# A streaming encoder step: one more gate pair by seven products, four convolution rows as filling, the last pair stored raw

## The chip, the cores and the metric

The kernel runs on one core of a Trainium2 chip. The metric is the device time of one execution in microseconds (us), lower is better. The median of three runs is 1542.54 us (1541.74 to 1542.68).

Engines by the profile's names: PE is TensorE (matmuls), PEld its weight load, DVE VectorE, ACT ScalarE, POOL GpSimd, SP SyncE, which issues the DMAs. Each works through its own instructions in order.

## The reference

One layer: a root-mean-square norm, one input projection whose columns feed an attention branch, a short convolution and two sets of sigmoid gates; the branches are merged by the gates, then an output projection, an MLP and a gated embedding follow. 1024 prompt rows and 32 sample rows (T = 1056), width 1024, all in float32.

```python
h = rmsnorm(x, g_mix)
proj = h @ w_in                     # columns: q k v cb cc cx (512 each), ga gc (1024 each)
q, k, v, cb, cc, cx, ga, gc = jnp.split(proj, SPLITS, axis=-1)
y_attn = attend(q, k, v).reshape(b, t, SB_WIDTH) @ w_attn_out
conv_out, new_buf = causal_conv(cc * cx, conv_buf, conv_w)     # width 3, per channel
y_conv = (cb * conv_out) @ w_conv_out
merged = jax.nn.sigmoid(ga) * y_attn + jax.nn.sigmoid(gc) * y_conv
x = x + merged @ w_o
...

def stick_breaking(q, k, v, q_pos, k_pos):
    z = jnp.einsum('bqhd,bkhd->bhqk', q, k) * scale
    mask = k_pos[None, :] < q_pos[:, None]
    log_1m = jnp.where(mask, jax.nn.log_sigmoid(-z), 0.0)
    tail = lax.cumsum(log_1m, axis=3, reverse=True) - log_1m
    a = jnp.where(mask, jnp.exp(jax.nn.log_sigmoid(z) + tail), 0.0)
    return jnp.einsum('bhqk,bkhd->bqhd', a, v)
```

## The kernel before

Activations lie with features on the partitions and the 1056 rows along the free axis. Every operand is split into a high and a low part, and each product of a weight block with an activation block is three matmuls: high by high, high by low, low by high. The high part is a cast on ACT, the low part a subtraction on DVE.

**Stages.** In-projection, attention (64 steps), branches, output projection, MLP (up, down), gated embedding. The change touches the first three. The norm's factor `rs` is multiplied in after the in-projection.

**In-projection.** The columns form blocks of 128, taken in pairs (a "set"): gates g0 to g15 (0 to 7 are the attention branch's, 8 to 15 the convolution branch's), q, k, v and the three convolution parts cb, cc, cx (four blocks each). Gates g0 to g3 come first, by plain products (`first_gates`). The sets from index 2 of `SETS` on go by seven products of half-size blocks in the place of eight (`seven`): 7 products x 2 column halves x 12 matmuls of 128x264 = 168 for a pair. A product is a step of the loop `run`; after each step, `run` lets every generator in `side` do one piece of its work. A set has 14 such steps. In `side` are: `prepare`, which forms the weight sums of the next set (four sums on POOL, L203) and splits them (L164 on ACT, L166 on DVE); the fetch of the set after; and what `follow` puts there once a set is done: scaling by `rs` (L482), for gates the sigmoid (L578) and the store to `gd` in DRAM (L579, `gate_done`), for cx and cb the steps of the convolution (`conv_in`: the product with cc, L539, the taps, L547 on ACT and L155 on DVE; `conv_gate`: L563, the cast L567, its low part L570). `follow` gives the second block of a pair a later start than the first, by a table of steps: six for cx, four for cb.

In `seven` the last product of a set (A22, `ps_A11i<-T,shA_i` in the profile) overwrites the PSUM tile that L257 on DVE reads, and its results are copied by ACT (L651).

**What is left of the gates is filling.** The six gate blocks that no set makes (10 to 15) are cut into pieces (`plan_gates`; a quarter of the columns of one block is 24 matmuls of 128x264 in four pieces, L659 to L661, its copy L663). Behind them in the plan stand the embedding products (`embed_pieces`, L752 to L754, copied by ACT at L755) and the first `CFILL` = 2 rows of the convolution branch (`conv_pieces`, L975 to L977, 36 matmuls of 128x352 a row, multiplied by the gate on DVE at L979). `START` = 3 units of the plan (72 matmuls) run between the in-projection and attention; the others are dealt to the attention steps by `shares`, which spreads the plan's total over the steps. A filling group takes one of two PSUM tiles.

**Attention.** A step n makes scores for 128 queries (L791, L792, into the one score tile `z`), reads them by a sigmoid on ACT (L795), masks on POOL (L802), scans on DVE (L809), transposes two steps later (L845, copied at L848 on ACT and L849 on DVE) and multiplies with the values (L866). `ORDER = "LSAFBFG"` is the order of these in a step; F is filling. At the last step the score tile becomes two more filling tiles (`zf`).

**Branches.** For each of the 8 rows of each branch that no filling made: 36 matmuls of 128x352, times the gate, merged. `READY` names the gates that are in DRAM scaled and with their sigmoid; for the others `branch_scale` and `branch_sigmoid` do it here (for the convolution branch the scaling is on POOL, for the attention branch on DVE).

PE, ACT, DVE and POOL run in the order in which the code is written (`manual_schedule`); SP's order is made by a scheduler. Buffers of `bpool` (34) serve nearly everything of size 128x1056.

Of the kernel before, what the change touches and what calls it, by code (L numbers as in the profile page):

```python
# [37 lines left out]
SHB = 4  # L38
AT1 = (5, 4, 6, 7, 8, 12)
AT_IN = (4, 8, 10, 12, 14, 18)  # L40
READY = (4, 5, 6, 7, 8, 9)
CFILL = 2
ORDER = "LSAFBFG"
START = 3
MM = {mybir.EngineType.Activation, mybir.EngineType.PE, mybir.EngineType.DVE, mybir.EngineType.Pool}
# [3 lines left out]
def tile_step(  # L49
# [8 lines left out]
    nc = tc.nc  # L58
# [79 lines left out]
    raws, ws, side = {}, {}, []  # L138
# [134 lines left out]
    def after(n, *gens):  # L273
        for _ in range(n):
            yield
        for g in gens:
            yield from g
# [12 lines left out]

    goff = (3 * SB + 3 * CW) // P
    coff = 3 * SB // P
    SETS = [("g", 0), ("g", 2)] + [(nm, 0) for nm in ("cc", "cx", "cb", "q", "k", "v")] + [("g", 4)]
    SETS += [(nm, 2) for nm in ("q", "k", "v")] + [("g", 6)] + [(nm, 2) for nm in ("cc", "cx", "cb")] + [("g", 8)]
    base = {"g": goff, "q": 0, "k": 4, "v": 8, "cb": coff, "cc": coff + 4, "cx": coff + 8}
    xw = [[blk(f"x{h}{j}", F32, [P, 2, TH]) for j in range(4)] for h in range(2)]

# [14 lines left out]
    def fetch_in(s_):  # L312
        nm, n = SETS[s_]
        fetch_pair(f"i{s_}", w_in, base[nm] + n)
# [113 lines left out]
    gd = dpool.tile([16, P, T], F32, name="gd")  # L428
# [153 lines left out]
    def follow(nm, n, ms, wait=0):  # L582
        gens = []
        for p, m in zip((n, n + 1), ms):
            if nm in "qk":
                gens.append(keys_or_queries(nm, p, m))
            elif nm == "v":
                gens.append(values(p, m))
            elif nm == "cc":
                cst["cc", p] = m  # L590
                gens.append(call(scaled, m))
            else:
                gens.append({"cx": conv_in, "cb": conv_gate, "g": gate_done}[nm](p, m))
        side.extend([after(wait, gens[0]), after(wait + {"v": 6, "cx": 6, "cb": 4, "g": 3}.get(nm, 1), gens[1])])

    def first_gates():

# [318 lines left out]
    def gate_ready(b):  # L916
        return b[1] + (8 if b[0] == "c" else 0) in READY

# [63 lines left out]
    def plan_rest():  # L982

        es = [(n, embed_pieces(n)) for n in range(KD)]
        cs = [(n, conv_pieces(n)) for n in range(CFILL)]
        e_, c_ = 4 * KD, 12 * CFILL
        i0, ne, nc_ = len(plan), 0, 0
# [17 lines left out]

    SEQ_B = [("c", CFILL)]
    for n in range(KD):
        SEQ_B += [("a", n), ("c", n + CFILL + 1)] if n < KD - CFILL - 1 else [("a", n)]

# [65 lines left out]
        for p in range(4):  # L1075
            nc.scalar.copy(sampled[1][p // 2][:, p % 2, PAST:], ksT[p])

    plan_gates([n for n in range(4, 16) if n not in READY])
    plan_rest()
    total = sum(size for size, _ in plan)  # L1080
    place, done = min(hooks), 0.0
# [27 lines left out]
    with tc.manual_schedule(engines=MM):  # L1109
        nc.scalar.preload_act_table_set("sqrt_and_others")  # L1110
        run(first_gates())
        for s_ in range(2, len(SETS)):
            nm, n = SETS[s_]
            if s_ == 2:
                side.append(after(1, stats_x()))
            elif s_ == 4:
                nc.scalar.preload_act_table_set("sigmoid_and_others")
            if s_ + 1 < len(SETS):
                side.append(prepare(f"i{s_ + 1}", AT_IN))
            else:  # L1120
                side.extend([after(4, second_parts(0)), after(6, second_parts(1)), after(4, call(hooks_to, -20)), after(10, call(hooks_to, 0))])
            if s_ + 2 < len(SETS):
                side.append(after(5, call(fetch_in, s_ + 2)))
            m = blk(f"m1_i{s_}"), blk(f"m2_i{s_}")
            run(seven(f"i{s_}", *m, copy_of))
            follow(nm, n, m, 6 * (s_ == 2))
        keys_values(0, 0)
        run(ahead(START))
        while side:
            run(range(1))  # L1130
# [97 lines left out]
    with tc.manual_schedule(engines=MM):  # L1228
        queries(0, 0, 0)
        queries(0, 0, 1)  # L1230
        for n in range(LAST + 3):
# [5 lines left out]
            if n < LAST:  # L1237
                i = steps[n][2]
# [671 lines left out]
    with tc.manual_schedule(engines=MM):  # L1910
# [35 lines left out]
        for u in range(ND):  # L1946
            v = u + 4
# [147 lines left out]
```

## Time and profile before

| what | us |
|---|---|
| median of three runs | 1542.54 |
| the profiled execution | 1542.94 |
| its span in the profile | 1541.1 |
| in-projection, up to the last product of the last set | 0 to 373.4 |
| attention, first scores to last values | 382.6 to 594 |
| DMA, mean busy share of 16 queues | 0.51 |

A row of a timeline has the start, the duration, the engine, the line, the operation, what is written and read, and in brackets how long the engine had been idle before it and what ended that. A row of groups has the count, the busy time with the mean in ns, and the idle time. A row of windows has the stretch, its length, each engine's busy time with its count of instructions, the granted PE clock (1.00 is full), the DMA share and GB/s. Matmuls overlap in the pipeline: one of 128x264 is listed with 0.28 us, while the next starts 0.12 us later. So PE's pace is read from starts and from counts.

### The profile page before, as it was taken

The page shows a single profiled execution, that of the slowest core. Times are in us where ns is not written, and L with a number is a line of the kernel's source. Part 1 is how long each engine was busy: PE and PEld are TensorE (multiplying, and loading weights), DVE is VectorE, ACT ScalarE, POOL GpSimd, SP SyncE. Part 2 cuts the span into 40 slices and gives each one's busy share as a digit, 9 for nine tenths or more (in the row PEclk, how much of TensorE's full clock was granted, in tenths as well). Part 3 has the DMA queues.
Part 4 walks back from the last instruction along what each step waited for, and adds up shares of the span by engine and source line. Part 5 has one row for each costly group of instructions (what it writes and reads, how often), then busy time and mean ns, then how long its engine had stood idle before and what let it go on. Part 6 is the DMA issues. An engine that isn't in the chain of part 4 may idle for free. (4 is left out here: it accounts for less than half of the span.)

```text
span 1541.1 us, 29464 instructions
## 1 busy us (share of the span) xinstructions
PE 1522.7 (99%) x11840; PEld 1511.4 (98%) x11840; DVE 1056.5 (69%) x1425; ACT 747.3 (48%) x1367; POOL 335.1 (22%) x342
## 2 busy tenths in 40 slices
PE   8999999999999999999999999999999999999997
PEld 8999999999999999999999999999999999999997
DVE  7568656656777887665577555445577986789756
ACT  6544444434555664322365555555643334434654
POOL 2123322230222232101312222222020220000253
PEclk9999999999999999999999999999999999999999
DMA  6513545415644843354354343444886897683443
GB/s 221 202 53 111 192 153 193 166 45 182 197 117 151 281 141 133 133 180 176 121 188 152 140 154 137 142 148 154 290 289 199 286 326 237 210 273 122 138 129 117
DMA packets 110569, 268.96 MB, mean 175 GB/s; under 512 B 12992, under 2 KB 30144, under 8 KB 110432
## 3 DMA queue, kind: packets, MB, share of 16 engines
q1 hardware_dynamic: 110144, 266.75, 51.2%
q8 instruction: 93, 1.52, 0.4%
q14 instruction: 44, 0.36, 0.1%
q10 hardware_dynamic: 288, 0.32, 0.1%
HBM read 186.31 MB, written 80.72 MB: 173 GB/s over the span
## 5 line engine op out<-in xcount | busy, mean ns | idle before, releaser
L1690 PE MATMUL ps_dn<-fh,whi_dn 128*128 128x264 f32 x896 | 254.7, 284 | 0.0
L1691 PE MATMUL ps_dn<-fl,whi_dn 128*128 128x264 f32 x896 | 254.5, 284 | 0.0
L1692 PE MATMUL ps_dn<-fh,wlo_dn 128*128 128x264 f32 x896 | 254.5, 284 | 0.0
L1692 PEld LDWEIGHTS ps_dn<-fh,wlo_dn 128*128 128x128 f32 x896 | 168.7, 188 | 0.0
L1691 PEld LDWEIGHTS ps_dn<-fl,whi_dn 128*128 128x128 f32 x896 | 168.5, 188 | 0.0
L1690 PEld LDWEIGHTS ps_dn<-fh,whi_dn 128*128 128x128 f32 x896 | 168.5, 188 | 0.0
L809 DVE TENSOR_TENSOR_SCAN r<-r 128x128 f32<-128x128 f32 (+3 forms) x64 | 86.6, 1353 | 5.6 <-POOL r L802 5.6
L203 POOL TENSOR_TENSOR s_i<-raw_i,raw_i 128x512 f32<-128x512 f32 x30 | 41.2, 1372 | 223.7 <-DVE slS_i L166 194.0
L203 POOL TENSOR_TENSOR s_u<-raw_u,raw_u 128x512 f32<-128x512 f32 x30 | 44.1, 1471 | 184.6 <-DVE slS_u L166 184.4
L1577 ACT CAST whi_dn<-raw_dn 128x1024 fp32r<-128x1024 f32 x40 | 42.1, 1051 | 84.7 <-PE ps_dn L1691 84.7
L802 POOL TENSOR_SCALAR_AFFINE_SELECT r<-r 128x128 f32<-128x128 f32 x64 | 40.1, 627 | 192.1 <-ACT r L795 192.1
L1583 DVE TENSOR_TENSOR wlo_dn<-raw_dn,whi_dn 128x1024 fp32r<-128x1024 f32 x40 | 61.3, 1531 | 28.5 <-ACT whi_dn L1577 28.5
L1774 POOL TENSOR_TENSOR xx<-xx,pgs 128x384 f32<-128x384 f32 (+1 forms) x23 | 24.3, 1058 | 216.4 <-DVE pgs L1773 209.8
L1603 DVE TENSOR_TENSOR fl<-mr,fh 128x1056 fp32r<-128x1056 f32 x56 | 70.0, 1249 | 0.3 <-ACT q L1643 0.3
L849 DVE TENSOR_TENSOR at<-pa,at 128x512 fp32r<-128x512 f32 (+2 forms) x96 | 51.9, 550 | 24.7 <-ACT at L848 24.2
L216 PE MATMUL ps_A11u<-T,shS_u 128*128 128x264 f32 x240 | 68.4, 285 | 0.0
L218 PE MATMUL ps_A11i<-T,slS_i 128*128 128x264 f32 x240 | 68.4, 285 | 0.0
L217 PE MATMUL ps_A11u<-T,shS_u 128*128 128x264 f32 x240 | 68.3, 285 | 0.0
L216 PE MATMUL ps_A11i<-T,shS_i 128*128 128x264 f32 x240 | 68.3, 285 | 0.0
L217 PE MATMUL ps_A11i<-T,shS_i 128*128 128x264 f32 x240 | 68.2, 284 | 0.0
L218 PE MATMUL ps_A11u<-T,slS_u 128*128 128x264 f32 x240 | 68.0, 283 | 0.0
L166 DVE TENSOR_TENSOR slS_i<-s_i,shS_i 128x512 fp32r<-128x512 f32 x45 | 36.1, 806 | 45.4 <-ACT shS_i L164 45.1
(451 smaller groups left out, 5607.8 us busy)
## 6 DMA issues: line engine op xcount, KB each, us to landing
raw_dn<-in_w_down_dram SPq DMA_DIRECT2D x56, 512.0 KB, 4.6
raw_i<-in_w_in_dram SPq DMA_DIRECT2D x34, 512.0 KB, 4.5
mr<-mdT SPq DMA_DIRECT2D x32, 528.0 KB, 5.7
raw_u<-in_w_up_dram SPq DMA_DIRECT2D x32, 512.0 KB, 3.6
mdB<-m SPq DMA_DIRECT2D x48, 264.0 KB, 2.4
mr<-mdB SPq DMA_DIRECT2D x24, 528.0 KB, 6.4
raw_pg<-in_w_ple_gate_dram SPq DMA_DIRECT2D x17, 512.0 KB, 3.6
mdT<-ta SPq DMA_DIRECT2D x32, 264.0 KB, 2.1
```

The source lines that it names most:

```text
L203: f()
L216: nc.tensor.matmul(p_, wh[:, k, :], o[:, 0, c], start=new and n == 0, stop=False, **on)
L217: nc.tensor.matmul(p_, wh[:, k, :], o[:, 1, c], start=False, stop=False, **on)
L218: nc.tensor.matmul(p_, wl[:, k, :], o[:, 0, c], start=False, stop=z, **on)
L809: nc.vector.tensor_tensor_scan(rev, rev, rev, 1.0, ALU.mult, ALU.bypass)
L849: nc.vector.tensor_tensor(al, pt[:, :nb, :], ah.bitcast(F32), op=ALU.subtract)
L1577: nc.scalar.copy(hi, dws[u])
L1583: dve(lo, raw, hi.bitcast(F32), op=sub)
L1603: dve(l, mraw.pop(v), opd[v].bitcast(F32), op=sub)
L1690: nc.tensor.matmul(ps, hi[:, j, :], oh, start=j == 0, stop=False)
L1691: nc.tensor.matmul(ps, hi[:, j, :], ol, start=False, stop=False)
L1692: nc.tensor.matmul(ps, lo[:, j, :], oh, start=False, stop=j == NP_ - 1)
```

## The change

The last gates in `SETS` are arranged anew: the set of g8 moves to the place where g4 stood, g10 takes the place of g8, and a further set, g4, is the last. `READY` becomes 6 to 11. The plan then makes gates 12 to 15 only, and four convolution rows in the place of two, so that the branch stage begins with row 4 of the convolution branch. The pair of the last set is written to `gd` as it leaves the products, without scaling and sigmoid; the branch stage does both for rows 4 and 5 of the attention branch. The second block of cx starts eight steps behind the first in the place of six, that of cb seven in the place of four.

```diff
-READY = (4, 5, 6, 7, 8, 9)
-CFILL = 2
+READY = (6, 7, 8, 9, 10, 11)
+CFILL = 4
...
-    SETS = [("g", 0), ("g", 2)] + [(nm, 0) for nm in ("cc", "cx", "cb", "q", "k", "v")] + [("g", 4)]
-    SETS += [(nm, 2) for nm in ("q", "k", "v")] + [("g", 6)] + [(nm, 2) for nm in ("cc", "cx", "cb")] + [("g", 8)]
+    SETS = [("g", 0), ("g", 2)] + [(nm, 0) for nm in ("cc", "cx", "cb", "q", "k", "v")] + [("g", 8)]
+    SETS += [(nm, 2) for nm in ("q", "k", "v")] + [("g", 6)] + [(nm, 2) for nm in ("cc", "cx", "cb")] + [("g", 10), ("g", 4)]
...
-        side.extend([after(wait, gens[0]), after(wait + {"v": 6, "cx": 6, "cb": 4, "g": 3}.get(nm, 1), gens[1])])
+        side.extend([after(wait, gens[0]), after(wait + {"v": 6, "cx": 8, "cb": 7, "g": 3}.get(nm, 1), gens[1])])
...
-    plan_gates([n for n in range(4, 16) if n not in READY])
+    plan_gates(range(12, 16))
...
             run(seven(f"i{s_}", *m, copy_of))
-            follow(nm, n, m, 6 * (s_ == 2))
+            if s_ + 1 < len(SETS):
+                follow(nm, n, m, 6 * (s_ == 2))
+            else:
+                for i in range(2):
+                    nc.sync.dma_start(gd[n + i], m[i])
```

**A convolution step in the in-projection.** On ACT, in the set that runs behind the first cx (names: `yc` is the convolution's sum, `ce` its edge, `shS` a weight's high part; numbers tell tiles apart), a piece of the difference:

```order
 L249 COPY u_i_1319<-ps_A11i_1_1345 128x264
-L547 ACTIVATE yc_1490<-m_i_787,vecT 128x1056
-L549 COPY ce_1488<-vecT 128x1 x2
-L550 COPY ce_1488<-m_i_787 128x2
-L164 CAST shS_i_1495<-raw_i_1_1191 128x512
-L164 CAST shS_i_1530<-s_i_1341 128x512
+L164 CAST shS_i_1485<-raw_i_1_1191 128x512
+L547 ACTIVATE yc_1520<-m_i_787,vecT 128x1056
+L549 COPY ce_1518<-vecT 128x1 x2
+L550 COPY ce_1518<-m_i_787 128x2
+L164 CAST shS_i_1525<-s_i_1341 128x512
```

The first weight cast has moved ahead of the convolution's taps. In the next set the same happens with the cast of the second conv gate (L567), which now stands behind the weight casts. There, DVE has, as a piece of the difference (`cvh` is that cast's output, `m_i` a set's result):

```order
+L108 TENSOR_TENSOR wlo_i_1675<-raw_i_0_1439,whi_i_1674 128x1024
+L570 TENSOR_TENSOR m_i_1314<-m_i_1314,cvh_1671 128x1056
+L252 TENSOR_TENSOR m_i_1577<-ps_A12i_0_1697,p_i_1579 128x264
+L252 TENSOR_TENSOR m_i_1577<-ps_A12i_1_1711,p_i_1580 128x264
 L482 TENSOR_TENSOR m_i_1315<-m_i_1315,rs 128x1056
-L108 TENSOR_TENSOR wlo_i_1676<-raw_i_0_1439,whi_i_1675 128x1024
-L570 TENSOR_TENSOR m_i_1314<-m_i_1314,cvh_1671 128x1056
-L563 TENSOR_TENSOR m_i_1315<-m_i_1315,yc_1490 128x1056
-L252 TENSOR_TENSOR m_i_1577<-ps_A12i_0_1699,p_i_1579 128x264
-L252 TENSOR_TENSOR m_i_1577<-ps_A12i_1_1713,p_i_1580 128x264
 L257 TENSOR_TENSOR m_i_1578<-ps_A11i_0_1585,s_i_1583 128x264
```

The scaling of the second block (L482) stands behind the split L108 and the additions L252, and its product with the convolution (L563) now follows behind the L257 shown.

**The start of attention.** On PE, from the first scores to the second (`z` scores, `ps_g` a gate group), before:

```order
L791 MATMUL z_4736<-ks_4612,q_4724 128x128
L792 MATMUL z_4736<-ks_4612,q_4724 128x128
L659 MATMUL ps_g_3_4744<-B_0_4525,whi_g_4564 128x264
L660 MATMUL ps_g_3_4744<-B_0_4525,whi_g_4564 128x264
L661 MATMUL ps_g_3_4744<-B_0_4525,wlo_g_4565 128x264
L659 MATMUL ps_g_3_4744<-B_1_4543,whi_g_4564 128x264
L660 MATMUL ps_g_3_4744<-B_1_4543,whi_g_4564 128x264
L661 MATMUL ps_g_3_4744<-B_1_4543,wlo_g_4565 128x264
L791 MATMUL z_4760<-ks_4612,q_4724 128x256
```

and now:

```order
L661 MATMUL ps_g_2_4915<-B_3_337,wlo_g_4802 128x264
L791 MATMUL z_4971<-ks_4853,q_4959 128x128
L792 MATMUL z_4971<-ks_4853,q_4959 128x128
L791 MATMUL z_4988<-ks_4853,q_4959 128x256
L792 MATMUL z_4988<-ks_4853,q_4959 128x256
L659 MATMUL ps_g_3_4996<-B_0_4764,whi_g_4801 128x264
```

The filling between the first two scores is gone. SP's queue there is now (`gd` the gates in DRAM, `vv` values, `q` queries):

```order
L1130 DMA gd<-m_i_4611 128x1056
L1130 DMA gd<-m_i_4612 128x1056
L765 DMA vv_4856<-vd 128x1024
L777 DMA q_4959<-qd 64x2x256
L778 DMA q_4959<-qd 64x256
L779 DMA q_4959<-qd 64x256
```

The two stores of the last pair stand ahead of the loads; before, the stores of the last pair (L579) stood behind all query loads of this place.

**Filling in mid-attention.** On PE at step 37 now (`ps_oc` a convolution group, `ps_pw` an embedding group):

```order
L977 MATMUL ps_oc_0_6575<-cv_6369,cw_6316 128x352
L752 MATMUL ps_pw_6651<-ph_6036,whi_pw_6222 128x264
L753 MATMUL ps_pw_6651<-pl_6037,whi_pw_6222 128x264
L754 MATMUL ps_pw_6651<-ph_6036,wlo_pw_6223 128x264
L752 MATMUL ps_pw_6651<-ph_6265,whi_pw_6222 128x264
L753 MATMUL ps_pw_6651<-pl_6266,whi_pw_6222 128x264
L754 MATMUL ps_pw_6651<-ph_6265,wlo_pw_6223 128x264
L975 MATMUL ps_oc_352_6659<-cv_6040,cw_6316 128x352
```

Where before at this step stood gate pieces alone, a convolution group ends, an embedding group follows, and the next convolution group begins directly behind it, in the PSUM tile of that embedding group.

## The prediction

> **What bounds the kernel now.** I read the page's head first, then the busy time by 40 us windows, then the timelines around the few places where TensorE stood still.
>
> ```profile
> span 1541.1 us, 29464 instructions
> PE 1522.7 (99%) x11840; PEld 1511.4 (98%) x11840; DVE 1056.5 (69%) x1425; ACT 747.3 (48%) x1367; POOL 335.1 (22%) x342
> 120.00:160.00 40.00, 39.18 (x319) 38.75 (x318) 36.52 (x42) 17.36 (x34) 13.43 (x8) 1.00 0.42 147
> 160.00:200.00 40.00, 40.00 (x331) 39.99 (x330) 24.53 (x34) 16.58 (x39) 12.10 (x8) 1.00 0.45 172
> 320.00:360.00 40.00, 40.00 (x329) 39.80 (x328) 27.49 (x40) 14.70 (x34) 6.04 (x4) 1.00 0.23 64
> 600.00:640.00 40.00, 40.00 (x249) 40.00 (x249) 26.83 (x37) 14.76 (x17) 9.25 (x5) 1.00 0.39 136
> ```
>
> PE is busy for 99% of the span and every other engine is well below it, so PE's own matmuls and its few pauses set the time. In the windows (window, length, PE, PEld, DVE, ACT, POOL busy with counts, granted clock, DMA share, GB/s) the undisturbed in-projection passes 331 matmuls of 128x264 in 40.00 us, **0.121 us each**; the branch stage passes 249 of 128x352, 0.161 us each. The window from 120 passes 12 fewer, that from 320 two fewer.
>
> **Term 1: fewer matmuls.** A gate pair in the plan is 2 gates x 4 quarters x 24 = 192 matmuls of 128x264; by seven products it is 7 x 2 x 12 = 168. So 24 x 0.121 = **-2.9 us**, the only firm term. The moves around it are sums of zero on PE: 168 matmuls (20.3 us) join the in-projection, 192 leave the attention (-23.2), and two convolution rows of 36 matmuls each (2 x 36 x 0.161 = 11.6) pass from the branch stage into the attention. What the new set prepares (four POOL sums, five splits) is what every set prepares, and 160-200 shows sets without a pause. So the attention has 23.2 - 11.6 = 11.6 us less filling.
>
> **Term 2: the start of attention.**
>
> ```profile
> 381.80:385.40 3.60, 2.20 (x16) 0.99 0.46 181
> 385.40:388.80 3.40, 3.40 (x16) 0.50 0.91 293
> 388.80:392.20 3.40, 3.40 (x29) 1.00 0.73 216
> 382.62 0.30 PE L791 MATMUL z<-ks,q 128*128 128x128 f32 x1 [0.52 <-issue]
> 382.76 0.28 PE L792 MATMUL z<-ks,q 128*128 128x128 f32 x1
> 384.70 0.39 PE L791 MATMUL z<-ks,q 128*128 128x256 f32 x1 [0.89 <-ACT r L795]
> 384.92 0.28 PE L792 MATMUL z<-ks,q 128*128 128x256 f32 x1
> 382.14 0.38 ACT L663 COPY sg<-ps_g 128x264 f32<-128x264 f32 x1 [2.53 <-PE ps_g L661]
> 382.42 2.06 ACT L578 ACTIVATE m_i<-m_i 128x1056 f32<-128x1056 f32 x2
> 384.38 0.27 ACT L795 ACTIVATE r<-z 128x128 f32<-128x128 f32 x1
> 385.24 0.38 ACT L795 ACTIVATE r<-z 128x256 f32<-128x256 f32 x1 [0.59 <-PE z L792]
> ```
>
> The windows here give PE alone. Two pauses, 0.52 and 0.89 us, and right behind them 3.4 us at half clock (16 matmuls in the place of 29), which costs 1.7 us. The first pause ends when the copy of the third gate group (382.14 + 0.38) has emptied the PSUM that the scores take over; this stays. The second: there is one score tile, its reader on ACT (384.38) stood behind the 2.06 us of sigmoids of the last pair. That pair now is stored raw, so they are gone from here. But the new order has no filling behind the first scores, so the next scores wait for the reader itself: it starts 0.32 us after the last score matmul starts (384.92 to 385.24), takes 0.27, and some 0.05 later PE goes on: 382.76 + 0.64 = 383.40, against a matmul end at 383.04, a pause of 0.36. Gain 0.89 - 0.36 = 0.53. Does the clock still drop? Before, 1.41 of 3.60 us were idle; now it would be 0.88. The end of attention (term 4) had a pause of 0.95 and stayed at full clock. I take no drop: 0.53 + 1.7 = **-2.2 us**; bounds -0.5 (it drops) and -2.6 (the 0.36 is hidden too).
>
> The Trainium skill, "TensorE: Matmul & The Clock Gate", What's actually happening, says that the clock falls to half after at least one idle window of about 3.4 us and that the windows run freely. The length agrees with the 3.4 us at 0.50; the cause doesn't, since the longest pause was 0.89 us. By its rule these pauses would not be the cause, the drop would stay and the term would be 0.5: the time of the first rival.
>
> On SP the two raw stores now stand ahead of the value and query loads.
>
> ```profile
> 373.38 0.55 SPq L777 DMA_DIRECT2D q<-qd  x1
> 373.38 0.38 ACT L651 COPY m_i<-ps_A11i 128x264 f32<-128x264 f32 x1 [1.11 <-PE ps_A11i L218]
> 383.53 1.85 SPq L579 DMA_DIRECT2D gd<-m_i  x2
> q<-qd SPq DMA_DIRECT2D x64, 64.0 KB, 2.9
> ```
>
> In the old times the last copy of a set ends at 373.38 + 0.38; one store has been issued by then, and the other (0.93), the value load and three query loads (0.55 each) are issued by 376.9, and land 2.9 later at 379.8: over 2 us before the scores can start at 382.5. It costs nothing; were both stores late, 1 us would still be left.
>
> **Term 3: the conv steps.**
>
> ```profile
> 117.44 1.18 ACT L547 ACTIVATE yc<-m_i,vecT 128x1056 f32<-128x1056 f32 x1 [5.58 <-DVE m_i L539]
> 119.44 0.69 DVE L166 TENSOR_TENSOR slS_i<-raw_i,shS_i 128x512 fp32r<-128x512 f32 x1 [1.75 <-ACT shS_i L164]
> 139.18 1.08 ACT L567 CAST cvh<-m_i 128x1056 fp32r<-128x1056 f32 x1 [4.12 <-DMA cvd<-cvh]
> 140.80 0.69 DVE L166 TENSOR_TENSOR slS_i<-raw_i,shS_i 128x512 fp32r<-128x512 f32 x1 [1.41 <-ACT shS_i L164]
> 141.41 0.42 DVE L257 TENSOR_TENSOR m_i<-ps_A11i,s_i 128x264 f32<-128x264 f32 x1
> 141.00 0.28 PE L218 MATMUL ps_A11i<-T,slA_i 128*128 128x264 f32 x1
> 141.89 0.39 PE L216 MATMUL ps_A11i<-T,shA_i 128*128 128x264 f32 x1 [0.61 <-DVE m_i L257]
> 134.81 1.23 DVE L108 TENSOR_TENSOR wlo_i<-raw_i,whi_i 128x1024 fp32r<-128x1024 f32 x1 [0.32 <-ACT whi_i L107]
> 124.78 3.40 DVE L166 TENSOR_TENSOR slS_i<-s_i,shS_i 128x512 fp32r<-128x512 f32 x2
> 355.36 1.29 DVE L166 TENSOR_TENSOR slS_i<-s_i,shS_i 128x512 fp32r<-128x512 f32 x2
> ```
>
> The last product of a set overwrites PSUM that L257 on DVE has to read; L257 stood behind a weight split (119.44, 140.80) that waited for ACT, and ACT stood in a conv step (117.44, 139.18). At place two PE's starts lie 0.89 us apart instead of 0.121. All places together cost what the windows lack: 12 + 2 matmuls, 14 x 0.121 = 1.7 us, of which 0.9 is place two with its restart. In the new order the split stands ahead of the conv step on ACT, so the others go: -0.8. At place two DVE has nearly the same work left ahead of L257: from the split at 134.81 (which waits for ACT, as before) 1.23 + 1.25 + 0.77 + 1.25 + 0.42 + 1.25 + 0.69 + 0.42, each overlapping its follower by 0.08, which ends at 141.5 instead of 141.83, for a need at 141.1. So half remains: -0.4. Against it, the second conv gates now run beside a set that is being prepared, which they did not: two splits of DVE took 3.40 us beside POOL's sums and 1.29 without. I give that the remaining half of place two, +0.5, and +0.2 for what else is late: **-0.5 us**, bounds -1.7 (all go) and +1.0 (place two stays, and the new set stalls twice as it did).
>
> The Trainium skill, "SBUF — State Buffer", SBUF: two separate sides, says that a DVE instruction with two SBUF inputs and a GpSimd instruction that reads SBUF lock each other out whole. The 3.40 against 1.29 agrees, and it speaks against this part of the change.
>
> **Term 4: attention with less filling.**
>
> ```profile
> 382.00:596.00 214.00, 211.31 (x1652) 203.49 (x1652) 170.54 (x235) 132.19 (x296) 53.38 (x131) 0.99 0.54 169
> 502.00:596.00 94.00, 92.72 (x701) 88.90 (x700) 82.03 (x116) 65.03 (x147) 24.55 (x55) 1.00 0.57 186
> L979 DVE TENSOR_TENSOR sc<-ps_oc,sc 128x352 f32<-128x352 f32 x5 | 2.6, 513 | 0.0
> L963 DVE TENSOR_TENSOR cw<-raw_oc,cw 128x512 fp32r<-128x512 f32 x2 | 1.4, 684 | 0.0
> 574.20 0.28 PE L754 MATMUL ps_pw<-ph,wlo_pw 128*128 128x264 f32 x1
> 575.03 0.39 PE L752 MATMUL ps_pw<-ph,whi_pw 128*128 128x264 f32 x1
> 582.35 0.39 PE L752 MATMUL zf<-ph,whi_pw 128*128 128x264 f32 x1 [0.95 <-ACT r L795]
> 583.83 0.43 PE L975 MATMUL zf<-cv,cw 128*128 128x352 f32 x1 [0.25 <-ACT em L755]
> ```
>
> DVE had 170.5 of 214 us. It gains two rows of 0.684 + 3 x 0.513 (4.4 us) and loses two gate splits (2 x 1.23): 172.4 of about 202, 85% instead of 80%. PE stays the longer engine, with thinner cover. A filling group needs a PSUM tile that was emptied: from the last matmul of one group (574.20) to the first that reuses its tile (575.03) went 0.83 us, though only three conv matmuls stood between. The new order has this at step 37 with nothing between: 0.83 - 0.12 = 0.7; elsewhere about as often as before: +0.5. Scores behind shorter filling: +0.2; scans that come late: +0.3; the 0.25 at 583.83 goes, since more stands ahead of it: -0.3. Together **+0.7 us**, bounds -0.5 and +3 (a quarter of the missing 11.6 us comes back as waiting).
>
> **Branches: 0.** The raw pair's scaling and sigmoid go to its two attention rows there; in 600-640 DVE has 26.83 of 40 us and ACT 14.76, and the number of rows that need them is ten before and after.
>
> **Sum.** -2.9 - 2.2 - 0.5 + 0.7 = -4.9 us. The profiled execution took 1542.94 (span 1541.1), 0.4 above the median of 1542.54: 1538.0 with the profiler, **1537.6 us** as the median is measured.
>
> **Rivals.**
> - *The clock still drops* (two pauses still lie within 1 us of each other, 0.88 us in all): 1.7 less gain, 1539.3. Chance 0.18.
> - *Less cover costs what it can:* term 4 at +3 with term 3 at +0.2: 1540.6. For it, DVE has 82.03 of 94 us in the last stretch; against it, PE's 92.72 of 94 there. Chance 0.14.
> - *DVE sets the pace of late attention; slower.* If DVE's 12.0 us of gaps from 502 on are waits that do not shrink, its 82.0 + 4.4 + 12.0 = 98.4 us takes the place of 94 less some 5 of filling: 9.4 us more, 1547.0. It decides once DVE's work and unavoidable gaps exceed about 89 us there; at 86.4 of work alone it is near, but PE had under 1.3 us of idle. Chance 0.05.
> - *The set saves nothing:* its steps stall as place two did on each of three products, 2.6 us: 1540.2. Nothing in 160-200 speaks for it. Chance 0.03.
>
> **How the numbers follow.** My forecast has 0.57, from 1536 to 1539.4; 0.03 is left for better (1535, all good bounds). For 8 in 10 the range takes in both middle rivals: 1535.4 to 1541.0. A difference of 0.2% (3.1 us) is about what a measurement can tell here: faster means below 1539.4. That has the forecast, the better case and half of the clock rival, with a little off for places I have not seen: 0.67. Within: the rest of it and the cover rivals, 0.27; slower 0.06.
>
> **What would show it.** Right: 24 fewer matmuls of 128x264; no half clock at the start of attention, and the second scores some 0.8 us behind the first; no ACT sigmoid of a gate pair there; full counts (331) around 100-160; attention near 203 us. Wrong: a window at 0.50 behind the start of attention; PE waiting on query loads; DVE near 95% with idle PE between 480 and 590; pauses of over 0.5 us in the last two sets of the in-projection.

## The result and the profile after

| kernel | median, us | lowest to highest | runs | profiled execution | its span |
|---|---|---|---|---|---|
| before | 1542.61 | 1541.23 to 1544.39 | 18 | 1542.94 | 1541.1 |
| changed | 1545.82 | 1544.19 to 1546.33 | 18 | 1546.33 | 1543.4 |

The ratio of the changed kernel to the one before is 1.0019, with a 95% interval of 1.0011 to 1.0026: slower by about 3 us, where 4.9 us faster was forecast, and above the upper end of the range (1541.0). The granted clock over the span is 0.996 in eight of the changed kernel's 18 runs (1545.82 to 1546.33 us), the profiled execution among them, and 0.997 or 0.998 in the other ten (1544.19 to 1545.82).

The head of the changed kernel's page:

```profile
span 1543.4 us, 29450 instructions
PE 1520.5 (99%) x11816; PEld 1508.0 (98%) x11816; DVE 1066.4 (69%) x1437; ACT 750.4 (49%) x1371; POOL 329.9 (21%) x344
```

PE has 24 matmuls fewer (11840 before) and is busy 2.2 us less, as the first term said. The span is 2.3 us longer all the same, so PE waits longer, or runs slower, somewhere. Starts of matmuls in the two traces say in which stage:

| stretch | before | changed | difference | forecast |
|---|---|---|---|---|
| up to the first scores | 382.62 | 402.98 | +20.4 | +20.3 (168 matmuls) - 0.5 |
| first scores to first output projection | 292.80 | 274.21 | -18.6 | -23.2 (192 matmuls) - 2.2 + 0.7 |
| from there to the last matmul | 857.81 | 858.37 | +0.6 | 0 |

The middle row is 6.1 us off, the first 0.6, the last 0.6. So most of the miss lies in the attention. Two windows of the in-projection and the whole-attention window (columns as before: PE, PEld, DVE, ACT, POOL, clock, DMA share, GB/s):

```profile
120.00:160.00 40.00, 39.62 (x323) 39.20 (x322) 36.27 (x40) 17.78 (x36) 14.54 (x8) 1.00 0.42 150
320.00:360.00 40.00, 40.00 (x330) 40.00 (x329) 28.42 (x38) 14.67 (x36) 11.82 (x8) 1.00 0.19 54
382.00:596.00 214.00, 208.96 (x1608) 200.25 (x1607) 168.95 (x237) 125.60 (x280) 44.11 (x128) 0.99 0.58 180
```

The stretches of the conv steps pass 323 and 330 matmuls (319 and 329 before): better, though not the full 331. The stretch from 382 to 596 holds the end of the in-projection here, so it isn't the same work as before; its use is the clock, still 0.99, although the half clock that the old trace has at the first scores isn't in this one.

The start of attention, PE's first and second scores, and the windows of PE around them:

```profile
402.98 0.30 PE L791 MATMUL z<-ks,q 128*128 128x128 f32 x1 [0.52 <-issue]
403.81 0.39 PE L791 MATMUL z<-ks,q 128*128 128x256 f32 x1 [0.42 <-ACT r L795]
```

```profile
402.40:406.00 3.60, 2.67 (x20) 1.00 0.80 230
406.00:409.40 3.40, 3.40 (x28) 1.00 0.95 258
```

The second scores stand 0.83 us behind the first, with a pause of 0.42, and the clock stays at 1.00: this is what term 2 described. The loss is at another place. PE's waits of over 0.9 us from 575 on, and the windows there with all engines:

```profile
588.04 0.66 PE L845 MATMUL pa<-ident,r 128*128 128x128 f32 x4 [1.11 <-DVE r L809]
590.04 0.39 PE L752 MATMUL ps_pw<-ph,whi_pw 128*128 128x264 f32 x1 [1.35 <-DVE sc L979]
597.36 0.39 PE L752 MATMUL zf<-ph,whi_pw 128*128 128x264 f32 x1 [1.40 <-ACT r L795]
```

```profile
584.00:587.40 3.40, 2.86 (x17) 2.15 (x15) 3.40 (x3) 2.04 (x5) 2.27 (x2) 1.00 0.38 158
587.40:590.80 3.40, 1.41 (x9) 1.18 (x10) 3.34 (x6) 1.07 (x2) 0.58 (x3) 0.95 0.01 1
590.80:594.20 3.40, 3.40 (x17) 3.35 (x17) 1.78 (x3) 0.18 (x1) 0.00 (x0) 0.54 0.00 0
```

Three pauses, 3.9 us in all, and behind the first two a window at 0.54. The old trace has one of them, 0.95 at the last. In the first two windows DVE is busy for 3.40 and 3.34 of 3.40 us: the engine that is 69% busy over the span is the bound for these 7 us. What it does there, then POOL and SP beside it:

```profile
580.68 1.22 DVE L809 TENSOR_TENSOR_SCAN r<-r 128x512 f32<-128x512 f32 x1
582.25 1.26 DVE L923 TENSOR_TENSOR sa<-sa,rs 128x1056 f32<-128x1056 f32 x1 [0.36 <-DVE r L809]
583.43 2.69 DVE L1258 TENSOR_TENSOR o2l<-oT,o2h 128x264 fp32r<-128x264 f32 x1
...
586.51 1.48 DVE L809 TENSOR_TENSOR_SCAN r<-r 128x640 f32<-128x640 f32 x1
...
589.48 0.52 DVE L979 TENSOR_TENSOR sc<-ps_oc,sc 128x352 f32<-128x352 f32 x1
...
582.59 3.23 POOL L923 TENSOR_TENSOR sc<-sc,rs 128x1056 f32<-128x1056 f32 x1
...
577.65 0.33 SPq L901 DMA_DIRECT2D sa<-gd  x1
```

And the same place in the kernel before, DVE:

```profile
568.59 1.23 DVE L923 TENSOR_TENSOR sa<-sa,rs 128x1056 f32<-128x1056 f32 x1
...
571.24 1.21 DVE L809 TENSOR_TENSOR_SCAN r<-r 128x512 f32<-128x512 f32 x1
572.37 0.40 DVE L1254 TENSOR_TENSOR o2l<-oT,o2h 128x264 fp32r<-128x264 f32 x1
...
573.16 1.48 DVE L809 TENSOR_TENSOR_SCAN r<-r 128x640 f32<-128x640 f32 x1
...
575.18 2.01 DVE L1254 TENSOR_TENSOR o2l<-oT,o2h 128x264 fp32r<-128x264 f32 x1
```

`sa` is the first attention gate of the branch stage, `sc` the first convolution gate; both are scaled here, ahead of their stage. Before, `sa` was scaled ahead of the scan of 128x512; now its load is issued so late (577.65, and 4.5 us to landing) that the scaling stands behind that scan and idles DVE for 0.36 us on top. The split of `o2l` behind it runs beside POOL's scaling of `sc` and takes 2.69 us in the place of 0.40. So from the end of the one scan to the start of the next pass 4.6 us, where 0.7 passed before. The kernel before has such a long split too (2.01 us, beside POOL's scaling from 573.19 to 576.90), but behind the scan of 128x640. In the code `sa` is scaled in `branches`, behind the attention; in both traces this runs among the attention's last scans, so for it the written order isn't the one that runs, and nothing in the diff names its place. The transposes (588.04) wait for the scan, the filling (590.04) for the product L979 on DVE, which stands behind the scan.

**Theory A**: this block on DVE is the loss. **Theory B**: PE has too little filling and waits somewhere, whatever DVE does. Both were put to the chip.

### The profile page after: what moved, and what is told of

The parts are those of the page before. It is cut to its first block, busy times and chain, and to the rows that moved or that the text cites. A ratio compares the mean times of both kernels' runs of the same rounds, so it can differ in the third digit from the quotient of the medians.

```text
span 1543.4 us, 29450 instructions
## 1 busy us (share of the span) xinstructions
PE 1520.5 (99%) x11816; PEld 1508.0 (98%) x11816; DVE 1066.4 (69%) x1437; ACT 750.4 (49%) x1371; POOL 329.9 (21%) x344
## 4 chain that ended last, share of the span: by engine, by line
PE 61%; ACT 0%; DVE 0%; issue 0%; DVEq 0%
PE ps_dn L1694 7%; PE ps_dn L1696 7%; PE ps_dn L1695 7%; PE ps_A11u L216 4%; PE ps_A11u L217 4%; PE ps_A11u L218 4%; PE ps_pg L116 2%; PE ps_pg L117 2%; PE ps_wo L1385 2%; PE ps_wo L1384 2%; PE ps_wo L1383 2%; PE ps_pg L118 2%; PE ps_S1u L216 2%; PE ps_S1u L217 2%; PE ps_S1u L218 2%; PE ps_oa L116 1%
## 5 line engine op out<-in xcount | busy, mean ns | idle before, releaser
L216 PE MATMUL ps_A11i<-T,shS_i 128*128 128x264 f32 x256 | 73.0, 285 | 0.0
L218 PE MATMUL ps_A11i<-T,slS_i 128*128 128x264 f32 x256 | 72.9, 285 | 0.0
L217 PE MATMUL ps_A11i<-T,shS_i 128*128 128x264 f32 x256 | 72.7, 284 | 0.0
L802 POOL TENSOR_SCALAR_AFFINE_SELECT r<-r 128x128 f32<-128x128 f32 x64 | 32.1, 502 | 189.5 <-ACT r L795 184.4
```

Source lines behind the costliest of these rows:

```text
L216: nc.tensor.matmul(p_, wh[:, k, :], o[:, 0, c], start=new and n == 0, stop=False, **on)
L217: nc.tensor.matmul(p_, wh[:, k, :], o[:, 1, c], start=False, stop=False, **on)
L218: nc.tensor.matmul(p_, wl[:, k, :], o[:, 0, c], start=False, stop=z, **on)
```

## The experiments

Each kernel was timed beside the kernel before on the same chip. Times are medians in us.

| run | this | before | ratio, 95% interval |
|---|---|---|---|
| e1_sa_late | 1544.26 | 1542.97 | 1.0009 (1.0000 to 1.0017) |
| e2_both_late | 1542.39 | 1542.97 | 0.9997 (0.9988 to 1.0006) |
| e3_conv_back | 1546.37 | 1542.97 | 1.0022 (1.0013 to 1.0030) |
| e4_raw_only | 1543.19 | 1542.97 | 1.0001 (0.9993 to 1.0010) |
| e5_place | 1542.22 | 1543.17 | 0.9995 (0.9987 to 1.0004) |
| e6_place_c3 | 1542.21 | 1543.17 | 0.9996 (0.9987 to 1.0005) |
| e7_place_sets | 1547.09 | 1543.17 | 1.0029 (1.0017 to 1.0040) |
| e8_place_start2 | 1546.56 | 1543.17 | 1.0028 (1.0017 to 1.0040) |
| e9_best | 1543.21 | 1543.18 | 1.0002 (0.9994 to 1.0011) |
| e10_best_c3 | 1544.73 | 1543.18 | 1.0011 (1.0002 to 1.0020) |
| e11_before_sa | 1543.49 | 1543.18 | 1.0004 (0.9995 to 1.0012) |
| e12_act_out | 1542.50 | 1542.48 | 1.0001 (0.9992 to 1.0010) |
| e13_act_out_both | 1540.63 | 1542.48 | 0.9987 (0.9978 to 0.9996) |

### The two scalings, taken away one after the other

e1, from the changed kernel (the scaling of `sa` goes behind the last scan):

```diff
         elif n == LAST + 1:
             branch_high(SEQ_B[0])
             branch_low(SEQ_B[0])
+            branch_scale(SEQ_B[1])
...
             if nxt:
-                branch_scale(nxt)
+                if i:
+                    branch_scale(nxt)
```

> As the changed kernel, but the scaling of the first attention gate (sa, 1.26 us of DVE, which stands ahead of a scan at 582) is done only after the last scan. Theory A (DVE is blocked at 582 to 586, by this scaling with its 0.36 us wait and by a split of 2.69 us that shares the time with POOL's scaling; PE's two pauses of 1.1 and 1.35 us there and the half clock behind them are its result): the pauses at 588 and 590 shrink by 1.6 in all, the clock stays at 1.00, the time falls by 2.5 to 4 to about 1542.5. Theory B (PE simply lacks filling, 11.6 us of it, and will wait somewhere in late attention whatever DVE does): within 1 us of 1545.8.

e2 has that and POOL's scaling of `sc` moved as well, with its sigmoid on ACT:

```diff
-        elif n == LAST - 4:
+        elif n == LAST:
             branch_scale(SEQ_B[0])
-        elif n == LAST - 2:
+        elif n == LAST + 1:
             branch_sigmoid(SEQ_B[0])
```

> As the one with the late sa, and POOL's scaling of the first convolution gate of the branch stage (sc, 3.23 us) is also moved behind the last select. Theory A: the split of 2.69 us falls to 0.4, no pause over 0.7 us between 580 and 592, no half clock, late attention as long as before the change less its filling: 4.5 us less, 1541.3. Theory B: 1545 or more.

The ratio falls from 1.0019 to 1.0009 and to 0.9997: 1.5 and 1.9 us. DVE and POOL in e1:

```profile
582.53 0.41 DVE L1260 TENSOR_TENSOR o2l<-oT,o2h 128x264 fp32r<-128x264 f32 x1
...
583.57 3.59 DVE L809 TENSOR_TENSOR_SCAN r<-r 128x640 f32<-128x640 f32 x1
...
583.36 2.46 POOL L923 TENSOR_TENSOR sc<-sc,rs 128x1056 f32<-128x1056 f32 x1
```

and DVE in e2:

```profile
583.71 0.41 DVE L1259 TENSOR_TENSOR o2l<-oT,o2h 128x264 fp32r<-128x264 f32 x1
...
584.75 1.48 DVE L809 TENSOR_TENSOR_SCAN r<-r 128x640 f32<-128x640 f32 x1
```

With `sa` away the split is short, but now the scan itself meets POOL's scaling and takes 3.59 us; PE's first pause is gone, the second is still 1.14 us. Only when POOL's scaling goes too do all have their own length, and both pauses are gone. So e1 gained less than its 2.5 to 4, since one victim of POOL's scaling followed the other. But e2 moves the sigmoid of `sc` as well, and in the changed kernel this stands on ACT just ahead of the scores' reader (596.28 to 597.30) that ends the third pause:

```profile
595.17 1.08 ACT L928 ACTIVATE sc<-sc 128x1056 f32<-128x1056 f32 x1
```

That pause is 1.41 us in e1 and 0.42 in e2. By the starts of the matmuls, e2 gains 1.4 us over e1 at the second pause and 1.0 at the third, and loses 0.5 behind them. So Theory A holds for DVE's block, but not all of the 3.4 us is DVE's: 1.0 is ACT's. Moving both isn't free: e2 has a pause of 0.66 us in front of the first branch group, where the moved scaling stands ahead of the last values on DVE.

The Trainium skill, "SBUF — State Buffer", SBUF: two separate sides, says that a DVE instruction with two SBUF inputs and a GpSimd instruction that reads SBUF exclude each other for a whole instruction. The rows agree: the split takes 2.69 us against 0.41, the scan 3.59 against 1.48; POOL's scaling began first each time, and they end 0.30 and 1.34 us behind it, a little less than their own length.

### The conv steps

e3: the changed kernel with the old distances.

```diff
-wait + {"v": 6, "cx": 8, "cb": 7, "g": 3}
+wait + {"v": 6, "cx": 6, "cb": 4, "g": 3}
```

> As the changed kernel, but the second blocks of cx and cb start 6 and 4 steps behind the first again. If the wider steps do what I forecast (0.5 us gained, the third of my terms), about 1546.3, and the pause of 0.4 to 0.9 us is back at each of the old places (120, 141). If they gain nothing or cost (the trace shows +0.2 for the whole in-projection against what its added products cost), 1545.3 to 1545.8.

It takes 1546.37, a ratio of 1.0022 against 1.0019: the intervals don't tell them apart. PE's rows do, first of e3, then of the changed kernel:

```profile
120.70 0.39 PE L216 MATMUL ps_A11i<-T,shA_i 128*128 128x264 f32 x1 [0.21 <-DVE m_i L257]
...
142.15 0.39 PE L216 MATMUL ps_A11i<-T,shA_i 128*128 128x264 f32 x1 [0.71 <-DVE m_i L257]
...
372.65 0.39 PE L216 MATMUL ps_A11i<-T,shA_i 128*128 128x264 f32 x1 [0.52 <-DVE m_i L257]
```

```profile
141.32 0.39 PE L216 MATMUL ps_A11i<-T,shA_i 128*128 128x264 f32 x1 [0.33 <-DVE m_i L257]
...
371.47 0.39 PE L216 MATMUL ps_A11i<-T,shA_i 128*128 128x264 f32 x1 [0.34 <-DVE m_i L257]
```

The wider steps take away the pause at 120 and half of that at 141, as forecast, 0.59 us of idle time. The third place, at 371, has its pause with both distances (0.52 and 0.34), so it doesn't come from them; the kernel before had none there. It is the second conv gate beside the set that is being prepared, which e7 below bears out.

### The raw pair alone

e4: the kernel before, with only the last pair (g8) stored raw.

```diff
-READY = (4, 5, 6, 7, 8, 9)
+READY = (4, 5, 6, 7)
...
-    plan_gates([n for n in range(4, 16) if n not in READY])
+    plan_gates([n for n in range(4, 16) if n not in READY + (8, 9)])
...
-            follow(nm, n, m, 6 * (s_ == 2))
+            if s_ + 1 < len(SETS):
+                follow(nm, n, m, 6 * (s_ == 2))
+            else:
+                for i in range(2):
+                    nc.sync.dma_start(gd[n + i], m[i])
```

> The kernel before with one part of the change: the last pair (g8) is stored raw, and its two scalings (DVE) and sigmoids (ACT) are done ahead of the two convolution rows in the attention. If the start of attention is worth what the two traces suggest (the half clock and a pause of 0.5 us go, 2.3 to 2.6 us) and the two scalings find room: 1540.2. If late attention gives it back (DVE gains 2.5 us there): 1542 to 1543.

1543.19 against 1542.97: nothing gained. In its trace the old wait of 0.89 at the second scores and the half clock are gone, and behind them it has gained 2.7 us on the old trace, by the starts of the matmuls. By 568 us, 2.4 of that is given back. In the list of PE's waits (what waits, for whom, us in total, times, the longest) there is a new entry:

```profile
PE ps_pw L752 <- ACT em L755: 1.4, 2, 0.9
```

The two waits are at 523 and 556, and on ACT the two sigmoids stand just ahead:

```profile
519.89 1.08 ACT L928 ACTIVATE sc<-sc 128x1056 f32<-128x1056 f32 x1
...
555.45 1.10 ACT L928 ACTIVATE sc<-sc 128x1056 f32<-128x1056 f32 x1
```

Done here, they make ACT late with the copies that empty the filling's PSUM tiles. In this kernel, the work that was taken off a stage's end came back where it is done instead.

### Better places, and what cover is worth

e5 moves `sc` one step less far (to `LAST - 1`, its sigmoid to `LAST`) and `sa` behind the first branch group:

```diff
             branch_post(b, 0)
+            if i == 0:
+                branch_scale(nxt)
+                branch_sigmoid(nxt)
```

> As the one with both scalings moved, but sc comes one step earlier (behind the last select) and sa only behind the first group of the branch stage, so that neither stands ahead of the end of attention (0.66 and 0.25 us of pauses at 607 and 604 there). Theory A (the two scalings were what term 4 lacked, and the rest of the forecast holds): 1 us less than with both moved, 1541.4; without the pause at 607, and none above 0.7 from 560 to 600.

1542.22: 0.8 above what was expected. The pause ahead of the branch stage is gone, but POOL's scaling of `sc` (593.29 to 595.73) now meets the split ahead of the last scan, which takes 2.26 us, and the transposes behind that scan wait 0.9. e6 is e5 with `CFILL = 3`, e8 is e5 with `START = 2`:

> As the one with the better places, with three convolution rows in the filling in the place of four: 5.8 us less filling in the attention, 5.8 more in the branch stage, where PE has no pauses. Theory B (cover is short: the pauses from 420 to 515 grew by 2.9 for 11.6 us of filling taken away): 1.5 us more than with four rows, 1542.9. Rival (the rows' four DVE operations each weigh more than their cover): the same or up to 1 less.

> As the one with the better places, with two units of filling ahead of the first scores in the place of three, so that the attention has 2.9 us more. Theory B: 0.25 of that comes back, 0.7 less, 1540.7. Rival: the first scores, 2.9 us earlier, wait for their queries, and it comes out the same or slower.

Three rows instead of four: 1542.21, no difference in the median; the runs of each spread over 1.6 and 2.1 us. So 5.8 us of filling less doesn't show the cost of 1.5: theory B, as a rule of so much wait for so much missing filling, isn't borne out. More filling (e8) made it 4.3 us slower. Two causes show among PE's waits in e8: the first scores, 2.3 us earlier, wait for their queries, and

```profile
PE ps_pw L752 <- DVE sc L979: 2.7, 2, 1.6
PE z L791 <- DMA q<-qd: 1.5, 1, 1.5
```

two filling groups wait for a PSUM tile that DVE has to empty. How much of the 4.3 each makes wasn't separated. In these runs more filling wasn't more cover: what counted was what its groups wait for.

### The order of the sets

e7 is e5 with g10 ahead of the second cc, cx, cb:

```diff
-    SETS += ... + [("g", 6)] + [(nm, 2) for nm in ("cc", "cx", "cb")] + [("g", 10), ("g", 4)]
+    SETS += ... + [("g", 6), ("g", 10)] + [(nm, 2) for nm in ("cc", "cx", "cb")] + [("g", 4)]
```

> As the one with the better places, with g10 ahead of the second cc, cx, cb, so that the second conv gates run beside the last set, which prepares no further set, as they did before the change. If the pauses of 0.5 to 1.2 us at 371 and 373 come from the conv gates beside a set that is prepared: they go, 0.5 to 1.2 less, 1540.6. If a set stalls there whatever follows the gates: the same as with the better places.

The pause at 371 is gone, and the kernel is 4.9 us slower than e5:

```profile
405.57 0.44 PE L791 MATMUL z<-ks,q 128*128 128x128 f32 x1 [3.44 <-DMA q<-qd]
```

The stores of the late conv gates now stand ahead of keys, values and queries on SP, and the first queries come 3.44 us late; the clock is at 0.50 for some 6.8 us behind that. e9 is e7 with the first queries loaded ahead of the raw stores and of the values, and the scaling of `sc` where e2 has it:

```diff
         queries(0, 0, 0)
         queries(0, 0, 1)
+        for i in range(2):
+            nc.sync.dma_start(gd[raw_pair[0] + i], raw_pair[1][i])
+        keys_values(0, 0, "v")
```

> The changed kernel with the places of both scalings (sc behind the last scan, sa behind the first branch group), g10 ahead of the second cc, cx, cb, and the first queries loaded ahead of the raw stores and of the values. If the 3.44 us wait for the first queries in the kernel with the other set order came from stores and values that lay ahead of them in the DMA queues: it goes, the half clock behind it too, and the in-projection keeps what it gained (1.4), late attention gains 1.0 against the better places: 1540.0. If the queries are late whatever stands ahead: 1545 or more.

> The same with three convolution rows in the filling. From the pair measured before (four rows 1542.22, three rows 1542.21) the number of rows is worth nothing: the same within 1. Theory B (cover): 1.5 more.

The wait of 3.44 and the half clock are gone (the first scores start at 403.22, at full clock), but e9 takes 1543.21, not 1540.0. One row of its trace shows where 1.6 us of that went, in the scores of the sample rows (`zs`):

```profile
410.51 2.31 PE L1165 MATMUL zs<-kk,qs 64*32 64x288 f32 x16
```

In e5 these 16 matmuls take 0.72. Here they wait for the cached keys `kk`, whose loads are issued from 405.78 on, behind the raw stores and the values; in e5 they are issued from 404.18 on, though its first scores are 0.8 later. The rest of the 3.2 us isn't settled. With three rows, e10, it is 1544.73; 1.3 us of that is a later wait for queries, the one at 408.81, which e9 doesn't have. Most of the difference between four rows and three lies here in those loads, so the pair says little of cover. No run with this order of the sets came below e5 or e13, which keep the order of the change.

### The same lateness without the rest of the change

e11 is the kernel before with one DVE instruction moved: `sa` is scaled behind the scan of 128x512.

```diff
             if nxt:
-                branch_scale(nxt)
+                if i:
+                    branch_scale(nxt)
...
                     if 1 <= n <= LAST:
                         weigh(*steps[n - 1])
+                    if n == LAST - 4:
+                        branch_scale(SEQ_B[1])
```

> The kernel before, with nothing changed but the place of one DVE instruction: the scaling of the first attention gate (sa, 1.23 us) stands behind the scan of 128x512 of the last block, where the changed kernel has it, and not one scan earlier. Theory A (the place alone blocks DVE there): the scan of 128x640 starts 1.2 to 2.5 later, PE waits, 1.5 to 4 more: 1544.5 to 1547. Rival (it needs the thinner filling as well): within 0.7 of before, 1543.

DVE's rows of e11, then PE's one:

```profile
571.37 1.28 DVE L923 TENSOR_TENSOR sa<-sa,rs 128x1056 f32<-128x1056 f32 x1
572.58 2.69 DVE L1257 TENSOR_TENSOR o2l<-oT,o2h 128x264 fp32r<-128x264 f32 x1
...
575.66 1.47 DVE L809 TENSOR_TENSOR_SCAN r<-r 128x640 f32<-128x640 f32 x1
...
577.19 0.66 PE L845 MATMUL pa<-ident,r 128*128 128x128 f32 x4 [0.74 <-DVE r L809]
```

The split is there to the hundredth (2.69), and the kernel loses only 0.3 us, within its interval. This understates the place itself: matmul by matmul against the trace of the kernel before, e11 falls back 1.0 us between 557 and 577. But at the first scores it has the same two pauses, 0.52 and 0.89, and no half clock behind them; PE's window there:

```profile
385.40:388.80 3.40, 3.40 (x28) 1.00 0.98 315
```

Even at 1.0, Theory A in its plain form (1.5 to 4) falls: by itself, DVE's lateness costs PE one pause of 0.74. In the changed kernel PE pauses twice, and the second pause is a filling group that waits for L979. That gave **theory C**: DVE's lateness reaches PE by two ways, the scan, and the filling's own PSUM tiles, since every convolution group is emptied by DVE (an embedding by ACT), and the changed kernel has twelve such groups in the place of six.

### Emptying the convolution groups on ACT

e12 is the changed kernel with both scalings where it has them; ACT copies each finished convolution group into a weight tile that is no longer needed, and DVE multiplies the copy. e13 has the moves of e1's kind as well (`sc` as in e2, `sa` as in e5).

```diff
                 if k == 3:
-                    dve(mg[n][:, c], ps, mg[n][:, c], op=ALU.mult)
+                    t_ = fetched["c", n][0].rearrange("p k c -> p (k c)")[:, :352]
+                    nc.scalar.copy(t_, ps)
+                    dve(mg[n][:, c], t_, mg[n][:, c], op=ALU.mult)
```

> The changed kernel, with the places of both scalings as it has them; only each finished group of the convolution rows is copied out of PSUM by ACT, and DVE multiplies the copy by the gate (48 us of filling, 12 more ACT copies of 0.5 us, the product in SBUF). Theory C (DVE's lateness at 582 to 588 reaches PE twice, once by the scan and once because the filling's own PSUM tile is emptied by DVE behind that scan; the moved scaling alone, in the kernel before, cost 0.9 us at the scan and nothing more): the pause of 1.35 at 590 goes, the first of 1.1 stays, no half clock, 3 us less: 1542.8. Rival (the scan's wait alone brings the half clock, or ACT's copies delay the scores): 1545 or more.

> The same copies by ACT, and both scalings moved away (sc behind the last scan, sa behind the first branch group). Theory C: with DVE no longer late at 582 to 588 the copies have little left to save; the pauses of 0.63 at 514 and 0.7 at 497 have other causes (ACT's copies of the embeddings): 1542 within 0.7. If convolution groups that wait for DVE cost elsewhere too: 1541 or less.

e12 comes to 1542.50, the forecast to 0.3. Its PE rows and windows at the place:

```profile
587.27 0.66 PE L845 MATMUL pa<-ident,r 128*128 128x128 f32 x4 [1.17 <-DVE r L809]
593.45 0.39 PE L752 MATMUL zf<-ph,whi_pw 128*128 128x264 f32 x1 [1.37 <-ACT r L795]
```

```profile
587.40:590.80 3.40, 3.40 (x26) 3.20 (x26) 3.37 (x5) 1.26 (x4) 0.31 (x3) 1.00 0.00 0
590.80:594.20 3.40, 2.03 (x15) 1.59 (x14) 3.37 (x6) 3.05 (x5) 0.56 (x1) 1.00 0.00 0
```

DVE is as late as in the changed kernel (3.37 of 3.40 us busy, the transposes wait 1.17), but the filling behind the transposes starts at once, and the clock stays at 1.00. From these transposes to the next scores pass 2.76 us (587.27 to 590.03), where the changed kernel took 5.92 (588.04 to 593.96): half of the difference is the pause, half the clock. e13, where DVE isn't late either, takes 1540.63: 0.13% less than before, with an interval of 0.04 to 0.22%. That is the second of the two cases expected, though its interval overlaps those of e2 and e5, and the copies are not all that sets it apart from e2: its waits are shorter by 0.5 at 514, by the copies, and by 0.7 ahead of the branch stage, by the place of `sa`. What is left of PE's waits from 380 to 605 in e13:

```profile
PE av L866 <- DVE at L849: 0.7, 1, 0.7
PE z L791 <- issue: 0.5, 1, 0.5
PE zf L752 <- ACT r L795: 0.4, 1, 0.4
PE z L791 <- ACT r L795: 0.4, 1, 0.4
PE ps_pw L752 <- ACT em L755: 0.3, 1, 0.3
```

That is 2.3 us, where the changed kernel has 6.2 (1.4 + 1.4 + 1.1 + 0.6 + 0.5 + 0.5 + 0.4 + 0.3). Beside the places at 582 to 597, a wait of 0.47 of a convolution group for its tile at 514 has gone. e13 is the one kernel here that beats both.

## Why the prediction was wrong, step by step

- **Term 1 (-2.9)** was right: 24 matmuls fewer.
- **Term 2 (-2.2)** was right in its mechanism for the pause: 0.89 became 0.42. The half clock isn't in the changed kernel's trace, as forecast, but its 1.7 can't be credited to the change: e11 has the old pauses and no half clock either, so the kernel before need not pay it in every run. And e4, which has this term alone, gained nothing: the raw pair's sigmoids cost ACT and PE about as much later. I had put them in the branch stage, which is true of the changed kernel, where the raw pair belongs to rows 4 and 5 of the attention branch.
- **Term 3 (-0.5)** was right in its mechanism and mis-sized. By the starts of the matmuls, the changed kernel gains 0.7 us from 34 to 351 us, at the old places, where I had summed 1.2. The second conv gates beside a set that is prepared took 0.7 back at 371, where I had allowed 0.5, and 0.2 for what else is late. That leaves nothing of the term, and it is most of the 0.6 us by which the in-projection is longer than forecast.
- **"Branches: 0" is the first step that failed.** I counted the rows that need scaling, ten before and after, and their stage, in which DVE and ACT have room. But two of these scalings, the first `sa` and the first `sc`, are done in the attention, and `sa` had moved from one side of a scan to the other, with a later load ahead of it. A moved instruction has to be priced where it stands: 1.26 + 0.36 us, and a split of 2.69 behind it, in front of a scan that PE waits for. By e11 this alone is 0.3 us in the medians and 1.0 in the traces.
- **Term 4 (+0.7, bounds -0.5 and +3)** is the step that made the rest. Its "scans that come late: +0.3" came out as the pauses of 1.11 and 1.35 and the half clock behind them: the matmuls from 590.04 to 593.96 take 3.92 us, and 2.34 in e12 at full clock. Its part on PSUM, a filling group that waits for its tile, was seen, but priced at the nearest row (0.83 us against 0.12); I took the reader to be prompt. It is an instruction in DVE's queue, and it is as late as whatever stands ahead of it. With that reader on ACT (e12), the second pause and the half clock are gone.
- **The half clock** has no place in term 4; a pause of 0.95 there had left it at full speed, and two pauses in one stretch were not among my cases at that place.
- **The rivals.** "DVE sets the pace of late attention" named the engine and the sign. Its mechanism, DVE's work and gaps summed over 94 us, isn't what happened: DVE has 168.95 of 214 us in the window from 382, no more than before (170.54, though 21 us of that window are in-projection now). It was the bound for 7 us. A sum over a stage can't show that.
- **The rest.** The stages behind the attention took 0.6 us more, and 0.9 in e5 and e13, while e6 took 0.5 less than before. No part of the change touches them, and no experiment was made on that; the cause stays open.

Put together from the starts in the traces: the miss is 7.2 us, 0.6 in the in-projection, 6.1 from the first scores to the output projection, 0.6 behind it. In e2 that middle stretch takes 269.76 (404.90 to 674.66), 4.4 less than in the changed kernel. The first two pauses (2.5) and the half clock (1.6) are gone, which is DVE's block; the third pause is 1.0 shorter, which is ACT's sigmoid; 0.7 comes back ahead of the branch stage. Another 1.4 of the miss are the waits at 430, 496 and 514 (0.65, 0.27 and 0.47) that the old trace doesn't have. The medians lie 3.2 apart, 0.9 more than the traces. Part of this lies outside the span: a run takes 1.7 to 1.9 us more than its span in the kernel before and 1.9 to 2.9 in the changed one, and what fills that isn't shown.

## What to carry to other kernels

Filling hides a late engine only if that engine doesn't also empty the filling's buffers: ask of each filling group which queue its PSUM tile waits in, and what stands ahead there. When an order changes, look for the few instructions that changed sides with one that the bound engine waits for, and price each at its new place, with what runs beside it; averages over a stage won't show them. Work that is put off at one stage's end has to be priced by a run with that edit alone. And a half clock seen in one trace isn't a price yet: look for a second trace of the same code.

## What the runs showed of the hardware

- **POOL's scaling held up each DVE instruction with two SBUF inputs that began behind it in the rows shown**, a scan as well as a subtraction: 0.41 to 2.69, 1.48 to 3.59, and in e12 the scaling of `sa` itself from 1.26 to 3.39 us. Where `sa` began first (582.25 against 582.59), it kept its 1.26, and POOL's scaling took 3.23 in the place of 2.46 (e1).
- **Short pauses can bring the half clock, and the same pauses need not.** 1.11 and 1.35 us of idle time within 3.1 us were followed by a window at 0.54, though PE had worked in between; 1.05 and 1.35 (e3) by some 6.8 us at half clock; 1.17 and 1.37 some 6 us apart (e12) left it at 1.00. At the first scores 0.52 and 0.89 were followed by 3.4 us at 0.50 in the trace of the kernel before, and by none in that of e11. A wait of 3.44 (e7) gave some 6.8 us at half clock, as the two short pauses of e3 did. What decides between these isn't shown. The Trainium skill, "TensorE: Matmul & The Clock Gate", What's actually happening, asks for at least one idle window of about 3.4 us. No pause near these half clocks but that of e7 is that long, so the measured rows speak against it; e7 agrees.
- **A load's place in the queue is worth as much as an engine's**: in e7 stores ahead of the first queries cost 3.44 us of wait and the half clock, while the DMA engines were busy without a break (a share of 0.94 to 1.13 in each microsecond from 400 to 404).
